# Three more places for the FFN's right operands, and a scratch of 4 KB for dynamic DMAs

## The chip, the cores and the metric

The kernel runs on one core of a Trainium2 chip. The engines are TensorE (PE, its weight loads listed apart as PEld), VectorE (DVE), ScalarE (ACT), GpSimd (POOL) and SyncE (SP, which issues nearly all DMAs). Each engine works through its own queue in order and waits on semaphores. The metric is the time of one execution on the device in microseconds (us); smaller is better.

## The reference

Two layers on a sequence of 1024 tokens with 1024 channels, all in float32. Layer 0 mixes with an mLSTM, layer 1 with a conformer convolution of 31 taps; each is followed by a gated FFN of 2816 channels with a convolution of 3 taps.

```python
c_act = silu(c)
for layer in range(2):
    mod = c_act @ ada_w[layer] + ada_b[layer]
    sh1, sc1, g1, sh2, sc2, g2 = split(mod, 6)
    h = modulate(rmsnorm(x, norm_mix_g[layer]), sh1, sc1)
    y = mlstm_block(h, ...) if layer == 0 else conformer_conv_block(h, ...)
    x = x + g1 * y
    h = modulate(rmsnorm(x, norm_ffn_g[layer]), sh2, sc2)
    x = x + g2 * conv_ffn(h, ...)
return rmsnorm(x, final_g)

def conformer_conv_block(h, ...):
    a, gte = split(h @ w_pw1 + b_pw1, 2)
    u = causal_dwconv(a * sigmoid(gte), dw_w, dw_b)
    return silu(layernorm(u, ln_g, ln_b)) @ w_pw2 + b_pw2

def conv_ffn(h, ...):
    gate, val = split(causal_dwconv(h @ w_up, conv_w, conv_b), 2)
    return (silu(gate) * val) @ w_down
```

## The kernel before

Channels lie on the 128 partitions, in blocks of 128 (`KB` = 8 blocks of the model, `FB` = 22 of the FFN); the 1024 tokens lie along the free axis, in two halves of 512 (`HS`). Every operand of a matmul is split into a high and a low part (`split`, L190: a cast on ACT at L191, a subtraction on DVE at L192), and a product is three matmuls (`PASS`). A split half of 128 x 512 is a tile `h` of 4 KB per partition; a split weight of 128 x 1024 is a tile `wu`. Plain weights (L220) run in the mLSTM, the conformer and a rest of the FFN's down-projection. In the FFN a two-by-two block of products is formed with seven products in place of eight (`Seven`, L507 and L926): its seven right operands are named b11, b21, t1, t3, b22, t2, t4 (`FORMS`), and `ORDER` is the order in which the seven products run, (0, 3, 2, 1, 6, 4, 5), which uses b11, t3, t1, b21, t4, t2, b22.

The stages follow one another: mLSTM (to about 760 us of the profile), FFN of layer 0 (to about 1545), conformer (to about 1934), FFN of layer 1, final norm. The code issues instructions in a program order; a scheduler then orders each engine's queue by priorities and by what it takes to be ready, and the built program holds that order. `tc.high_priority(n)` moves a piece ahead in it. The convolution's taps on DVE (L1725) have `LPC` = -100, so other work of DVE that is ready goes before them.

Memory: pools are put on the left or the right end of the core's SBUF and are closed again. A new tile may be written when the work on what lay at its addresses is over, and a pool that lies on the addresses of an older one makes its first writers wait for the older one's last readers. The scratch for dynamic DMAs is at the bottom of SBUF, 16 KB per partition by default, and all left pools lie above it. POOL issues the DMAs that use it, loads of the band matrices `wband` (L1658).

Three places matter here.

The FFN's right operands. `hx` (L700) has `3 * HALF` = 12 places for tiles `h`; `hpool` has 16. In the up-projection, the 28 tiles of the seven operands fill both. The down-projection's operands are the FFN's own channels, taken in chunks of eight blocks, four pairs. When a product of the last up-projection (L881) or of the last column of a chunk (L944) is issued, `release` (L676) returns the four places of its right operand, and as soon as seven places are free, `forms` (L681) loads one pair (its halves from `p_d`, its sums from `t_d`) and splits its seven operands. `ra` and `rb`, the tiles for the sums, exist once each. Later, `last` (L904) and `place` take further places from the same list.

The adaLN products. `ada_product` (L152) loads 512 KB of `ada_w` and reduces them on DVE (L155 and L156, 128 x 1024) to a column of `mod`; `adas` adds the bias (L162). The last 16 products of layer 1, whose results the FFN of layer 1 needs, run in the conformer from a pool `ca` on the right (`crep1` and two tiles `ada`), which is opened at L1782 behind the conformer's pool `conf`. In the profile these 16 products stand in the second pointwise convolution (pw2, from about 1830 us).

The residual input. `mlstm_down` (L1570) opens `x` again on the right and loads eight blocks (L1575); the right end of the left pools `m2` and `m2w` lies there before.

In the conformer, `cU` (L1677) is a convolution input that goes through a DRAM buffer (`u_d`, L1681 and L1683) to tiles `u` for the convolution on PE (L1703); the other blocks are convolved by the taps on DVE into `cy0` to `cy3`. L1621 and L1629 are the sums of the layer norm, L1633 its root, L1637 its scaling for pw2. L502 is the residual, L272 and L281 the sums of squares of the next norm.

Of the kernel before, what the change touches and what calls it, by code (L numbers as in the profile page):

```python
# [79 lines left out]
def trunk(ctx, tc, a):  # L80
    nc = tc.nc
# [10 lines left out]
    def phase(name, bufs=1, side=None):  # L92
        return tc.tile_pool(name=name, bufs=bufs, side=side, reuse_waits="tile")
# [3 lines left out]
    def nm(s):  # L97
        uid[0] += 1
        return f"{s}_{uid[0]}"
# [149 lines left out]
    class Norm:  # L249
        PARTS = HALVES  # L250

        def __init__(self, x, layer, which):
            self.x, self.layer, self.which = x, layer, which
            self.acts = [[], []]
            self.r = [None] * len(self.PARTS)
            self.squared = [0] * len(self.PARTS)
# [381 lines left out]
    class Operands:  # L638
# [4 lines left out]
        def __init__(self, p_d, t_d, hx):  # L643
            self.p_d, self.t_d, self.hx = p_d, t_d, hx
            self.kept = None
            self.free, self.places, self.right = [], [{}], [None]

        def sums(self, j, g, spare):

# [22 lines left out]
        def release(self, name):  # L672
            self.free += self.places[-2].pop(name)
            right = self.right[-1]
            while len(self.free) >= len(self.FORMS) and len(right["t4"]) < CHUNK // 2:
                self.forms(CHUNK * (len(self.right) - 2) + 2 * len(right["t4"]))  # L676

# [14 lines left out]
    HALF = KB // 2  # L692
    LATER = 16
    CHUNK = 8
    REST = FB - 2 * CHUNK

    def ffn(layer, normed, following, side, other):
        p_d = [dpool.tile([P, S], F32, name=nm("p_d")) for _ in range(FB)]
        with ExitStack() as es_h:
            hx = es_h.enter_context(phase(nm("hx"), 3 * HALF, side=side))  # L700
            t_d = [dpool.tile([P, 2, S], F32, name=nm("t_d")) for _ in range(CHUNK)]
            ops = Operands(p_d, t_d, hx)
            with ExitStack() as es_u:
                ux = es_u.enter_context(phase(nm("ux"), side=side))
                down = ffn_up(layer, normed, p_d, hx, ux, es_u, other, ops)
            open_x(other)
            for k in range(KB):
                dma(x_[0][:, k, :], normed.spill[:, k, :])
            ffn_down(layer, down, p_d, ops, following, other)

    def ffn_up(layer, normed, p_d, hx, ux, es_u, other, ops):
# [21 lines left out]
        def evacuate(j, s, q):  # L733
# [10 lines left out]
            def ready(name, at):  # L744
# [8 lines left out]
                if len(s.ready) == 4:  # L753
                    v.tensor_tensor(s.gate, s.gate, s.val, ALU.mult)
                    dma(p_d[j], s.gate)
                    if j < 2 * CHUNK:
                        ops.sums(j, s.gate, s.val)
# [138 lines left out]
    def ffn_down(layer, forms, p_d, ops, following, other):  # L896
        x = x_[0]
        gate = lambda m: mod[:, layer, 40 + m : 41 + m]
        with phase(nm("dx"), side=other) as dx:
# [4 lines left out]
            def last(h):  # L904
                j = FB - REST + len(acts[h])
                r = raw_tile()[:, :HS]
                dma(r, p_d[j][:, h * HS : (h + 1) * HS])
                t, _ = ops.take()
                split(r, t[:, 0], t[:, 1])
                acts[h].append(t)  # L910
# [4 lines left out]
            for c in range(2):  # L915
                right = ops.right[-1]
                if c == 0:
                    ops.add()
                s = Seven(forms, right, CHUNK // 2)
                s.banks[:4] = [ps() for _ in range(4)]  # L920
# [12 lines left out]
                for m in range(0, KB, 2):  # L933
# [3 lines left out]
                    for n, q in enumerate(ORDER if m else (0, 1, 2, 3, 6, 4, 5)):  # L937
# [16 lines left out]
                        elif q in (1, 6, 5):  # L954
                            ws.load(1 + (1, 6, 5).index(q))
                            if q == 5:
                                ops.free.sort(key=lambda pool: pool is hpool)
                                for _ in range(REST):
                                    last(0)
# [23 lines left out]
            os = [ps() for _ in range(lead)]  # L983
            for k in range(REST):
                for i in range(lead):
                    proj_k(os[i], ws.tiles[i], acts[0], k, REST)
            for h, (c0, c1) in enumerate(LAST if layer == DEPTH - 1 else HALVES):
                for m in range(KB):
# [5 lines left out]
                    following(h, m)  # L994
                    if not h and m >= 1 and len(acts[1]) < REST:
                        last(1)
# [950 lines left out]
```

## Time and profile before

| | us |
|---|---|
| three runs | 2614.78, 2617.64, 2620.78 |
| median | 2617.64 |
| profiled execution | 2619.32 |
| its span, from first to last instruction | 2617.5 |

In the profile a row of a timeline has start, duration, engine, line, operation, output and inputs, shape, count, and in brackets the idle time before it with what released it. A row of a group has line, engine, operation, tiles, shape and count, then busy us and the mean of one in ns, then the idle time before these instructions and its releasers. A row of a stretch has its bounds and length, then busy us (and instructions) of PE, PEld, DVE, ACT and POOL, the clock that PE was granted (1.00 is full), the DMA engines' busy share and GB/s. A DMA row has its queue, count, KB each, and the median us from issue to landing. The mean granted clock of the execution is 0.985.

### The profile page before, as it was taken

What the parts mean: (1) busy time and instruction counts of PE and PEld (TensorE: products, weight loads), DVE (VectorE), ACT (ScalarE), POOL (GpSimd) and SP (SyncE); (2) the same over time, 40 slices, a digit from 0 to 9 for tenths busy, and PEclk for the clock granted to TensorE, in tenths of its full rate; (3) what the DMA queues carried; (4) which work ended last, traced back from release to release, by engine and by line L of the source; (5) the groups of instructions that cost most, each with busy time, mean ns of one, the idle gap of its engine ahead of it and who ended that gap; (6) DMA issues with size and microseconds to landing.
All of it is one profiled execution on the core that took longest, in us unless ns stands there. A gap on an engine that the chain in (4) does not pass through costs nothing.

```text
span 2617.5 us, 31554 instructions
## 1 busy us (share of the span) xinstructions
PE 2501.1 (96%) x11421; PEld 2044.4 (78%) x11421; DVE 2203.5 (84%) x3064; ACT 1329.6 (51%) x2005; POOL 177.4 (7%) x320
## 2 busy tenths in 40 slices
PE   6999899999999999999999999999798999999998
PEld 4788688788778778888877888877576888887787
DVE  8988986787867899998889679992889998888866
ACT  6544445776634554444544342458564444444434
POOL 0232201332100000000000000000000000000000
PEclk9999899999999999999999999999999999999999
DMA  8676355432676234433354331545823332336422
GB/s 306 191 216 206 120 201 185 132 114 70 217 271 215 93 133 161 153 117 101 116 199 148 121 140 50 171 148 165 264 85 117 121 117 101 109 97 219 151 81 97
DMA packets 149085, 393.85 MB, mean 150 GB/s; under 512 B 14848, under 2 KB 36544, under 8 KB 148928
## 3 DMA queue, kind: packets, MB, share of 16 engines
q1 hardware_dynamic: 144320, 372.95, 43.0%
q0 software_dynamic: 4608, 18.88, 2.2%
q8 instruction: 90, 1.47, 0.2%
q14 instruction: 67, 0.55, 0.1%
HBM read 299.46 MB, written 92.31 MB: 150 GB/s over the span
## 4 chain that ended last, share of the span: by engine, by line
PE 67%; DVE 18%; DMA 6%; ACT 6%; issue 3%; SPq 0%; DVEq 0%; ACTq 0%
PE ps L507 41%; PE ps L220 19%; DVE cy L1725 5%; DVE h L192 3%; PE ps L1448 2%; PE ps L1485 2%; DVE wu L192 2%; DMA ada<-in_ada 1%; ACT cy L1712 1%; DMA raw<-xc_d 1%; ACT h L191 1%; PE ps L1102 1%; DMA raw<-p_d 1%; DVE ada L156 1%; ACT wu L191 1%
## 5 line engine op out<-in xcount | busy, mean ns | idle before, releaser
L507 PE MATMUL ps<-h,wu 128*128 128x512 f32 x4704 | 1098.5, 392 | 20.5 <-DVE wu L192 6.8
L507 PEld LDWEIGHTS ps<-h,wu 128*128 128x128 f32 x4704 | 884.1, 189 | 219.9 <-DVE wu L192 10.2
L220 PE MATMUL ps<-h,wu 128*128 128x512 f32 (+1 forms) x2574 | 608.3, 392 | 13.2 <-ACT h L191 6.2
L220 PEld LDWEIGHTS ps<-h,wu 128*128 128x128 f32 x2574 | 480.3, 190 | 122.6 <-ACT h L191 7.8
L191 ACT CAST wu<-raw 128x1024 fp32r<-128x1024 f32 (+1 forms) x286 | 298.4, 1045 | 299.6 <-PE ps L220 89.5
L192 DVE TENSOR_TENSOR wu<-raw,wu 128x1024 fp32r<-128x1024 f32 (+1 forms) x286 | 346.8, 1213 | 69.6 <-ACT wu L191 68.8
L840 DVE SCALAR_TENSOR_TENSOR c<-u,par,c 128x1024 f32<-128x1024 f32 x176 | 219.9, 1279 | 2.5 <-ACT c L838 2.4
L838 ACT ACTIVATE c<-u,par 128x1024 f32<-128x1024 f32 x88 | 108.5, 1243 | 107.5 <-DVE u L627 98.2
L507 PE MATMUL ps<-h,w 128*128 128x512 f32 x648 | 157.3, 390 | 1.9 <-DVE w L192 1.9
L1725 DVE SCALAR_TENSOR_TENSOR cy<-cu,par,cy 128x512 f32<-128x512 f32 (+1 forms) x180 | 156.0, 926 | 1.1 <-ACT cy L1721 0.3
L507 PEld LDWEIGHTS ps<-h,w 128*128 128x128 f32 x648 | 121.5, 188 | 28.0 <-DVE w L192 2.8
L502 DVE SCALAR_TENSOR_TENSOR x<-ps,mod,x 128x512 f32<-128x512 f32 (+1 forms) x140 | 97.9, 715 | 43.3 <-PE ps L220 35.5
L192 DVE TENSOR_TENSOR h<-raw,h 128x512 fp32r<-128x512 f32 (+1 forms) x160 | 105.1, 688 | 25.1 <-ACT h L191 24.9
L191 ACT CAST h<-raw 128x512 fp32r<-128x512 f32 (+1 forms) x160 | 91.4, 605 | 64.7 <-DMA raw<-p_d 28.1
L1448 PE MATMUL ps<-q,h 128*128 128x512 f32 (+2 forms) x576 | 115.3, 349 | 0.3 <-DVE q L192 0.3
L1448 PEld LDWEIGHTS ps<-q,h 128*128 128x128 f32 x576 | 94.9, 189 | 16.0 <-ACT t L1513 2.0
L156 DVE SCALAR_TENSOR_TENSOR ada<-ada,crep 128x1024 f32<-128x1024 f32 x69 | 83.0, 1215 | 22.4 <-DMA ada<-in_ada 22.1
L750 ACT ACTIVATE c<-c 128x1024 f32<-128x1024 f32 x44 | 46.7, 1061 | 94.6 <-DVE c L840 94.5
L728 POOL MEMSET u<- 128x2 f32 x88 | 8.4, 99 | 1123.4 <-DVE c L840 686.6
L220 PE MATMUL ps<-h,h 128*128 128x512 f32 (+1 forms) x450 | 83.6, 347 | 0.0
L220 PEld LDWEIGHTS ps<-h,h 128*128 128x128 f32 x450 | 72.4, 189 | 10.5
L1703 PEld LDWEIGHTS ps<-u,wband 128*128 128x128 f32 x576 | 66.9, 195 | 4.1 <-issue 3.7
(282 smaller groups left out, 3240.0 us busy)
## 6 DMA issues: line engine op xcount, KB each, us to landing
raw<-in_fup SPq DMA_DIRECT2D x94, 512.0 KB, 3.6
ada<-in_ada SPq DMA_DIRECT2D x85, 512.0 KB, 4.6
p_d<-c SPq DMA_DIRECT2D x44, 512.0 KB, 2.7
raw<-in_pw SPq DMA_DIRECT2D x40, 512.0 KB, 3.8
wband<-in_w POOLq DMA_DIRECT2D x32, 576.0 KB, 5.5
raw<-in_mup SPq DMA_DIRECT2D x32, 512.0 KB, 4.4
raw<-in_fdownS SPq DMA_DIRECT2D x32, 512.0 KB, 4.2
raw<-in_mdown SPq DMA_DIRECT2D x24, 512.0 KB, 4.4
```

The lines of the kernel that those rows point to most:

```text
L156: v.scalar_tensor_tensor(w, w, 1.0, crep, ALU.mult, ALU.mult, accum_out=mod[:, layer, b : b + 1])
L191: sc.copy(out_hi, raw)
L192: (engine or v).tensor_tensor(out_lo, raw, out_hi.bitcast(F32), ALU.subtract)
L220: pe.matmul(o, t[:, i, c : c + P], acts[k][:, j, :], start=k == 0 and n == 0, stop=k == nk - 1 and n == 2,)
L502: v.scalar_tensor_tensor(xs, o, gate, xs, ALU.mult, ALU.add)
L507: pe.matmul(o, w[:, i, k * P : (k + 1) * P], acts[k][:, j, :], start=first and k == 0 and q == 0, stop=last and k == n - 1 and q == 2, ski ...
L838: sc.activation(c, body(b), AF.Identity, scale=taps[FK - 1], bias=pv("fcb", layer, b))
L840: v.scalar_tensor_tensor(c, u[b][:, i : i + S], taps[i], c, ALU.mult, ALU.add)
L1448: pe.matmul(so[:, tlo:], xr[cc][I // nJ][:, i, I % nJ * P : (I % nJ + 1) * P], un["qs"][cc][:, j, tlo:], start=n == 0, stop=n == 3 * CB - 1,)
L1485: pe.matmul(un["num"][cc][:, tlo:], vr[I][:, i, cc * P : (cc + 1) * P], pt[:, j, tlo:], start=I == 0 and n == 0, stop=I == nJ * (hf + 1) - ...
L1703: pe.matmul(o, wd[:, 4 * d : 4 * d + 4, :].rearrange("p d c -> p (d c)"), phases[j][:, g, n0 + d : n0 + d + N4], start=d == 0, stop=d == 8,)
L1725: v.scalar_tensor_tensor(y, u[:, t + c0 : t + c1], pv("dww", t, j), y, ALU.mult, ALU.add)
```

## The change

`Operands` starts with three free places of `hx`, the pool `hx` has three places more, and the program is built with a scratch for dynamic DMAs of 4 KB per partition instead of 16.

```diff
-            self.free, self.places, self.right = [], [{}], [None]
+            self.free, self.places, self.right = [hx] * SPARE, [{}], [None]
...
     CHUNK = 8
+    SPARE = 3
     REST = FB - 2 * CHUNK
...
-            hx = es_h.enter_context(phase(nm("hx"), 3 * HALF, side=side))
+            hx = es_h.enter_context(phase(nm("hx"), 3 * HALF + SPARE, side=side))
...
-    nc = bacc.Bacc("TRN2", target_bir_lowering=False, num_devices=1)
+    nc = bacc.Bacc("TRN2", target_bir_lowering=False, num_devices=1, dynamic_dma_scratch_size=4096)
```

The three places take 12 KB per partition, as much as the scratch gives up. Outside the FFN all left pools lie 12 KB lower than before and the right ones stay: `conf`, which reached from 132320 to 189408, ends at 177120, and `ca` begins at 179936, so the two share no address any more. `x` of `mlstm_down`, from 194528 on, no longer lies on the last tiles of `m2` (they end at 184288 instead of 196576), only on `m2w`. Every engine has the same instructions as before in another order; POOL's order is the same too. From line 696 on the new code's numbers are one higher.

DVE at the start of the conformer, before: `gb` is a small product of `mod`, `cu` an input of the taps (L1695), `cy` the taps' sums (L1725), `wu` and `h` are splits.

```order
L1613 TENSOR_TENSOR gb_12592<-mod,par 128x8
L1695 SCALAR_TENSOR_TENSOR cu_12603<-ps_12421,par,t_1873_12601 128x512
L292 SCALAR_TENSOR_TENSOR h_12551<-t_1869_12549,mod,h_12551 128x512
L292 SCALAR_TENSOR_TENSOR h_12562<-t_1871_12560,mod,h_12562 128x512
L192 TENSOR_TENSOR wu_12617<-raw_12615,wu_12617 128x1024
L1695 SCALAR_TENSOR_TENSOR cu_12603<-ps_12423,par,t_1875_12606 128x512
L192 TENSOR_TENSOR wu_12684<-raw_12682,wu_12684 128x1024
```

The same place now, to the first tap:

```order
L156 SCALAR_TENSOR_TENSOR ada_14470,mod<-ada_14470,crep_14433 128x1024
L1614 TENSOR_TENSOR gb_12592<-mod,par 128x8
L156 SCALAR_TENSOR_TENSOR ada_14473,mod<-ada_14473,crep_14433 128x1024
L292 SCALAR_TENSOR_TENSOR h_12551<-t_1869_12549,mod,h_12551 128x512
L292 SCALAR_TENSOR_TENSOR h_12562<-t_1871_12560,mod,h_12562 128x512
L1696 SCALAR_TENSOR_TENSOR cu_12603<-ps_12421,par,t_1873_12601 128x512
L162 TENSOR_TENSOR mod<-mod,par 128x2
L156 SCALAR_TENSOR_TENSOR ada_14478,mod<-ada_14478,crep_14433 128x1024
L156 SCALAR_TENSOR_TENSOR ada_14481,mod<-ada_14481,crep_14433 128x1024
L192 TENSOR_TENSOR wu_12617<-raw_12615,wu_12617 128x1024
L1696 SCALAR_TENSOR_TENSOR cu_12603<-ps_12423,par,t_1875_12606 128x512
L192 TENSOR_TENSOR wu_12684<-raw_12682,wu_12684 128x1024
```

Four of the 16 adaLN products stand there; six more follow among the first six taps, and the last six stand at the end of the taps. Their loads stand on SP directly behind the writes of `x_d`.

DVE in pw2, before: `t` is the layer norm's scaled output, `h` its split form, `x` the residual.

```order
L1637 SCALAR_TENSOR_TENSOR t_2113_14632<-cy_12584,par,csc_12594 128x512
L156 SCALAR_TENSOR_TENSOR ada_14491,mod<-ada_14491,crep_14433 128x1024
L502 SCALAR_TENSOR_TENSOR x_14428<-ps_14606,mod,x_14428 128x512
L156 SCALAR_TENSOR_TENSOR ada_14494,mod<-ada_14494,crep_14433 128x1024
L1637 SCALAR_TENSOR_TENSOR t_2115_14638<-cy_12585,par,csc_12594 128x512
L162 TENSOR_TENSOR mod<-mod,par 128x2
L192 TENSOR_TENSOR h_14635<-t_2113_14632,h_14635 128x512
L192 TENSOR_TENSOR wu_14709<-raw_14707,wu_14709 128x1024
L156 SCALAR_TENSOR_TENSOR ada_14554,mod<-ada_14554,crep_14433 128x1024
L192 TENSOR_TENSOR h_14641<-t_2115_14638,h_14641 128x512
```

The same place now:

```order
L1638 SCALAR_TENSOR_TENSOR t_2113_14632<-cy_12584,par,csc_12594 128x512
L192 TENSOR_TENSOR wu_14653<-raw_14651,wu_14653 128x1024
L1638 SCALAR_TENSOR_TENSOR t_2115_14638<-cy_12585,par,csc_12594 128x512
L1638 SCALAR_TENSOR_TENSOR t_2122_14682<-cy_12586,par,csc_12594 128x512
L1638 SCALAR_TENSOR_TENSOR t_2124_14688<-cy_12587,par,csc_12594 128x512
L192 TENSOR_TENSOR h_14635<-t_2113_14632,h_14635 128x512
L502 SCALAR_TENSOR_TENSOR x_14428<-ps_14606,mod,x_14428 128x512
L192 TENSOR_TENSOR h_14641<-t_2115_14638,h_14641 128x512
```

No adaLN product is left there.

DVE near the end of layer 0's up-projection (about 1280 us in the profile before), now: `w` and `wu` are split weights, the three `h` are the first operands of the down-projection's first pair, split from loads `t`, `raw` and `ra`. Before, the first of them stood nine rows behind `wu_10498`.

```order
L192 TENSOR_TENSOR w_1540_10495<-t_1539_10490,w_1540_10495 128x512
L192 TENSOR_TENSOR h_10568<-t_1548_10560,h_10568 128x512
L192 TENSOR_TENSOR h_10571<-raw_10561,h_10571 128x512
L192 TENSOR_TENSOR h_10574<-ra_10562,h_10574 128x512
L192 TENSOR_TENSOR wu_10473<-raw_10471,wu_10473 128x1024
L569 TENSOR_TENSOR raw_10471<-t_1539_10490,raw_10471 128x512
L570 TENSOR_TENSOR raw_10471<-raw_10471 128x512
L192 TENSOR_TENSOR wu_10498<-raw_10476,wu_10498 128x1024
```

Of the four pairs of a chunk the first three now follow the products with b11, t1 and t4 where they followed those with t3, b21 and t2; the fourth still follows the last release, that of b22. The same holds between the two chunks of the down-projection, and in layer 1.

At the end of the mLSTM, SP's first load of `x` (L1575) stands before the loads of `hn` and `xc` for the operands of block 5, the other seven behind those of block 7; before, all eight stood behind those of block 9. Three of DVE's residuals L502 stand between the splits of those operands.

## The prediction

> **What bounds the kernel now.** I read the page first, then its chain of waits, then a table of stretches, then the timelines of TensorE and VectorE where a stretch is not full.
>
> ```profile
> span 2617.5 us, 31554 instructions
> PE 2501.1 (96%) x11421; PEld 2044.4 (78%) x11421; DVE 2203.5 (84%) x3064; ACT 1329.6 (51%) x2005; POOL 177.4 (7%) x320
> PE 67%; DVE 18%; DMA 6%; ACT 6%; issue 3%; SPq 0%; DVEq 0%; ACTq 0%
> ```
>
> TensorE (PE) is busy 96%, so a change of order can win only its idle time, 116.4 us in all, and the time at a lower clock; it can lose by making PE wait. Of the other third of the chain more than half is VectorE (DVE). The places that this change touches are these:
>
> ```profile
> 1299.00:1335.00 36.00, 30.83 (x119) 22.98 (x118) 33.38 (x47) 19.82 (x30) 0.00 (x0) 0.91 0.74 245
> 1380.00:1412.00 32.00, 30.05 (x125) 22.41 (x125) 30.23 (x46) 20.75 (x35) 0.00 (x0) 1.00 0.67 222
> 1650.00:1660.00 10.00, 7.17 (x47) 6.70 (x46) 10.00 (x12) 4.01 (x7) 0.71 (x2) 0.83 0.33 103
> 1760.00:1830.00 70.00, 66.23 (x385) 56.41 (x384) 22.41 (x26) 52.53 (x93) 4.32 (x9) 0.98 0.45 141
> 1830.00:1900.00 70.00, 53.22 (x193) 37.52 (x191) 57.22 (x90) 37.55 (x50) 0.13 (x2) 0.90 0.80 265
> 2360.00:2402.00 42.00, 35.97 (x139) 27.05 (x138) 37.79 (x53) 22.15 (x33) 0.00 (x0) 0.91 0.76 259
> ```
>
> The columns are PE, PEld, DVE, ACT, POOL busy, then PE's clock, DMA share, GB/s. The first and the last row are the step from up- to down-projection of the two FFNs: PE idles 5.2 and 6.0 us while DVE is 93% and 90% busy. From 1830 to 1900 (pw2 of the conformer) PE idles 16.8 us. At 1650 DVE is full and PE waits; from 1760 on DVE is two thirds idle.
>
> **The change part by part.** Instructions stay the same in number and kind; their order moves. All sums are against the profiled execution (2619.32 us, 1.7 above the median of 2617.64), and I take the difference off the median.
>
> *1. Sixteen products L156 leave the pw2 stage.* The pool `ca` no longer lies on `conf`, so its loads and products needn't wait until the conformer's pools close. Ten now stand at the start of the convolution, six behind most taps.
>
> ```profile
> L156 DVE SCALAR_TENSOR_TENSOR ada<-ada,crep 128x1024 f32<-128x1024 f32 x16 | 19.5, 1218 | 6.4 <-DMA ada<-in_ada 6.3
> L502 DVE SCALAR_TENSOR_TENSOR x<-ps,mod,x 128x512 f32<-128x512 f32 x10 | 7.2, 743 | 0.0
> L192 DVE TENSOR_TENSOR h<-t,h 128x512 fp32r<-128x512 f32 x8 | 5.5, 685 | 0.0
> 1831.78 6.02 PE L220 MATMUL ps<-h,wu 128*128 128x512 f32 x24
> 1837.63 5.31 PE L1629 MATMUL ps<-t,ones 128*128 128x512 f32 x12
> 1845.02 23.24 PE L220 MATMUL ps<-h,wu 128*128 128x512 f32 x100
> 1883.27 4.33 PE L220 MATMUL ps<-h,wu 128*128 128x512 f32 x16 [1.55 <-DVE h L192]
> 1898.67 2.08 PE L281 MATMUL ps<-acc,ones 128*128 128x512 f32 x2 [11.07 <-DVE acc L272]
> 1899.75 34.64 PE L220 MATMUL ps<-h,wu 128*128 128x512 f32 x144
> ```
>
> The group rows are of the window 1830 to 1900. There DVE spends 19.5 us on the products and 6.4 us waiting for their loads, 25.9 in all, and PE's L281 waits for DVE. Without them I ran the new DVE order by hand with the durations of these rows (h split 0.69, residual 0.74; a weight split is 1.22 in the row of 1564 below): the second half's last h split ends at 1868.9, the last sum that L281 needs at 1875.7. PE's own work from 1831.78 is 168 L220 at 0.227 (38.1) and 16 L1629 at 0.45 (7.3), so it gets to L281 at 1877.2 at the earliest, against 1898.67. That is 21.4 us at best. Not less than 16.8, if only the idle time of the stretch goes; I take **20**, as DVE is ready 1.5 us ahead of PE in the hand run, and waits for ACT within the stage will cost about as much.
>
> *2. The ten products are now ahead of the taps.* DVE has little room there:
>
> ```profile
> 1564.34 1.22 DVE L192 TENSOR_TENSOR wu<-raw,wu 128x1024 fp32r<-128x1024 f32 x1 [3.57 <-ACT wu L191]
> 1558.69 0.75 DVE L1695 SCALAR_TENSOR_TENSOR cu<-ps,par,t 128x512 f32<-128x512 f32 x1 [0.57 <-ACT t L1687]
> 1612.05 13.25 DVE L1725 SCALAR_TENSOR_TENSOR cy<-cu,par,cy 128x1024 f32<-128x1024 f32 x11
> ada<-in_ada SPq DMA_DIRECT2D x16, 512.0 KB, 4.8
> 1645.20 1.17 DVE L1677 SCALAR_TENSOR_TENSOR cU<-ps,par,t 128x512 f32<-128x512 f32 x1
> 1653.76 9.78 PE L1703 MATMUL ps<-u,wband 128*128 128x128 f32 x72 [2.83 <-DMA u<-u_d]
> ```
>
> Ahead of the first L1677, on which the first band convolution on PE (L1703) hangs through two DMAs, stand ten products more (12.2), four small biases L162 (an estimated 0.6) and four taps (4.8: eleven in a row take 13.25): 17.6 us. The idle time ahead of the taps (3.57 and 0.57) takes up some; with two `ada` tiles, each third product waits 4.8 us for its load, so by hand only 2.9 is taken up, and L1677 ends at about 1661 instead of 1646.4. PE waited there already, so nothing covers it: the wait of 2.83 grows to about 17. Queued behind it on PE is the rest of the convolution and pw1. The later L1677 have no taps more ahead of them than before, so they are only 8 to 10 us late, and PE, being 14 to 15 late, no longer waits for them. It gets back about 1 of the idle time at 1752, nothing from the 3.77 at 1807, whose work hangs on PE itself:
>
> ```profile
> 1752.09 5.40 PE L1629 MATMUL ps<-t,ones 128*128 128x512 f32 x8 [2.17 <-ACT t L1628]
> 1807.32 10.11 PE L220 MATMUL ps<-h,wu 128*128 128x512 f32 x36 [3.77 <-ACT h L191]
> ```
>
> The six later products cost 7.3 us where DVE has 47.6 of 70 free (1760 to 1830): nothing, unless the last taps become late, which have that whole stretch. Loss **13**, bounds 9 (all idle time filled, the two waits absorbed) and 17 (none filled). Steps 1 and 2 together: **7 faster**, bounds 0 and 12.
>
> A new wait of 14 us also lets the clock fall. The row of 1650 to 1660 shows 0.83 after a wait of 2.83, and the 144 L220 behind the 11.07 took 34.64 where 144 at 0.227 are 32.7. By these rows a long wait costs 1.9 behind it; the old one goes and a new one comes: nothing.
> The Trainium skill ("TensorE: Matmul & The Clock Gate", What's actually happening) says that PE falls to half rate after an idle window of about 3.4 us and needs as long a busy one to return. By it the cost behind a wait is an estimated 1.7, for one of 11 us as for one of 17; the trace's 1.9 agrees, and the slow clock after 2.83 shows that the window's phase counts too.
>
> *3. The FFN's right operands come one release earlier.* With three places free from the start, the first release already frees seven, so `forms` of a pair runs one product earlier, for the first three of the four pairs.
>
> ```profile
> 1282.71 1.23 DVE L192 TENSOR_TENSOR wu<-raw,wu 128x1024 fp32r<-128x1024 f32 x1 [1.60 <-ACT wu L191]
> 1318.13 0.49 PE L926 MATMUL ps<-h,wu 128*128 128x512 f32 x1 [0.37 <-ACT h L191]
> 1320.22 0.73 PE L926 MATMUL ps<-h,wu 128*128 128x512 f32 x2 [1.60 <-DVE h L192]
> 1321.35 0.51 PE L926 MATMUL ps<-h,wu 128*128 128x512 f32 x1 [0.39 <-ACT h L191]
> 1323.83 1.65 PE L926 MATMUL ps<-h,wu 128*128 128x512 f32 x3 [1.98 <-DVE h L192]
> L192 DVE TENSOR_TENSOR h<-rb,h 128x512 fp32r<-128x512 f32 x8 | 5.1, 684 | 1.0 <-ACT h L191 1.0
> L192 DVE TENSOR_TENSOR h<-ra,h 128x512 fp32r<-128x512 f32 x7 | 4.6, 684 | 0.4 <-ACT h L191 0.4
> L926 PE MATMUL ps<-h,wu 128*128 128x512 f32 x36 | 12.1, 447 | 4.3 <-DVE h L192 3.6 <-ACT h L191 0.8
> ```
>
> The group rows are of 1299 to 1335. Three splits (0.6 pitch, 1.8) now fill DVE's gap of 1.60 at 1281, the next pair's loads start sooner, and the gaps of 0.4 and 1.0 that ACT's casts left go. So DVE is about 3 us ahead when L926 begins. In the hand run the four waits of the rows (4.3) vanish, but a wait of about 3 comes for the last pair, which cannot start before the last release and has two weight splits and four taps ahead of it; PE leaves the step 5 us sooner, part of it from fewer matmuls at the low clock. I take half of what is hand-won as lost to landings that I can't see: **3 us per FFN**, and 0.5 each from the same step between the two halves of the down-projection (the stretch from 1380, PE idle 2.0). 7 in all; bounds 0 (the last pair sets the end as now) and 12.
>
> *4. The end of the mLSTM.* `x` no longer lies on the last double weight, so its eight loads stand up to 15 places earlier on SP's queue, seven of them between the loads of `hn` and `xc` for the last operands, and three residuals L502 stand between the splits.
>
> ```profile
> 726.77 0.50 PE L220 MATMUL ps<-h,vr 128*128 128x512 f32 x1 [1.67 <-ACT h L191]
> 753.92 11.41 PE L220 MATMUL ps<-h,wu 128*128 128x512 f32 x49 [1.07 <-DVE wu L192]
> x<-in_x SPq DMA_DIRECT2D x8, 512.0 KB, 9.1
> ```
>
> Against it: three residuals at 0.74, and loads that land later because one of 512 KB goes before them (an eighth of 9.1, 1.1 us) and seven more behind. For it: seven matmuls now stand ahead of the one that waited 1.67, and the split behind the 1.07 no longer waits for a residual. **0**, bounds 3 either way.
>
> *5. The smaller scratch.* It serves the DMAs that POOL issues, the 32 loads of `wband`.
>
> ```profile
> q0 software_dynamic: 4608, 18.88, 2.2%
> wband<-in_w POOLq DMA_DIRECT2D x32, 576.0 KB, 5.5
> L1658 POOL DMA_DIRECT2D wband<-in_w x20 | 10.5, 527 | 195.7 <-PE ps L1703 195.7
> ```
>
> The last row is of 1557 to 1760: POOL waits for PE to free a buffer, not the other way. Cost nothing; were this cover gone, 5.5 us for a load, bound 10 for two in a row.
>
> **Sum.** Conformer 7, FFNs 7, mLSTM 0: 14 us. 2619.3 becomes 2605.3, and from the median 2617.6 comes 2603.6, **2604**.
>
> **The rivals.** *No change (2613 to 2621):* the stall at L1703 is 17 and pw2 gives 17, and in the FFNs the last pair's operands set the end as now, since neither its release nor its DVE work moves. For it speaks that each hand-won microsecond of step 3 hangs on loads into `ra` and `rb`, of which there is one tile each; against it, that DVE has the 1.60, 1.0 and 0.4 to fill and that L926 waits four times for operands which now stand ahead.
> *Slower (about 2623):* ScalarE is the next bound of pw2. Every h form needs a Silu, a cast and then DVE's split, and each sum for L281 a square, all on ACT, which is busy 37.55 of the 70 us. If L281 moves up by only 8 (its 11.07 less some 3 for a residual, a square and a sum in a row), the conformer is 13 - 8 = 5 slower, and with no gain in the FFNs the kernel is at 2623. It decides where pw2 gives less than 13 and the FFNs' gain does not make up the rest. Against it: the 16 products and their waits take 25.9 us off the very engine that L281 waits for, and ACT has 32 us free.
> *The scratch throttles (2620 to 2640):* if a quarter of it holds too few descriptors for the `wband` loads in flight, each L1703 group waits for its own load, up to 5.5 us for each group that isn't covered: four uncovered make 22, and the sum turns to 8 slower. POOL's waits for PE in the row speak against it.
> The Trainium skill ("DMA: Bandwidth & Descriptors", Terms) has these descriptors of 16 bytes written to rings in SBUF, so a smaller ring holds fewer. By it and the 144 packets of a load (4608 / 32), spread over 16 engines, a load is an estimated 144 bytes per engine and direction, and some fourteen loads fit in 4 KB if both directions share it. No run here shows a full ring.
> *The change doesn't do what it says:* excluded for the order, which the rows of the change show; that a place is free and its use is no earlier is the first rival.
>
> **How the numbers follow.** Forecast 0.64, no change 0.20, slower through ACT 0.10, throttled 0.04, and 0.02 for more than 26 us gained. The forecast alone covers 2592 to 2612: 26 is the conformer's 12, the FFNs' 12 and 2 of the mLSTM's 3. The range reaches on to 2618, which takes in three quarters of the first rival and leaves about 2 in 10 outside. A measurement of this kernel tells 0.2% (5.2 us) from no change; the bounds are 2612.4 and 2622.9. Faster is the forecast, the 0.02 and a fifth of the first rival, some of the forecast's own tail taken off: 0.70. Slower is half of the ACT rival, the throttle and a tail of the first: 0.12. Same: 0.18.
>
> **What would show it.** Step 1: no `ada` product between the second half's L1637, L281 some 3 us or less behind the L220 ahead of it. Step 2: ten products between 1557 and 1590, L1677 about 14 us later after the end of the FFN, the wait of the first L1703 at about 17 instead of 2.83, and the other L1703 waiting for nothing. Step 3: the first L192 h of an FFN's last step 13 us sooner, waits of L926 before the last pair gone, the windows of 36 and 42 us shorter by 3 each. Step 4: L220 with `vr` without its wait of 1.67, and L201's weight split not later than before. Wrong would be the prediction if L1703 waits less than 9 or more than 17, if L281 still waits over 6, or if a wait for `wband` shows on PE.

## The result and the profile after

| | us |
|---|---|
| before, median of 4 runs | 2617.51 (2614.78 to 2620.78) |
| the change, median of 4 runs | 2598.85 (2596.91 to 2602.11) |
| ratio, 95% interval | 0.9933 (0.9917 to 0.9949) |
| the change, profiled execution | 2596.91 |
| the change again, on another chip, 5 runs | 2598.65, ratio 0.9936 (0.9924 to 0.9948) |

The change gains 18.7 us (13 to 22 by the interval); 14 were forecast. The ratio is an estimate from all runs of both kernels, not the quotient of the two medians. The two profiled executions lie 22.4 us apart, more than the medians, so what is read from this one pair of traces comes out somewhat too large. The page of the changed kernel answers to the first rows of before:

```profile
span 2595.1 us, 31542 instructions
PE 2489.0 (96%) x11421; PEld 2041.0 (79%) x11421; DVE 2200.3 (85%) x3064; ACT 1328.9 (51%) x2005; POOL 171.3 (7%) x320
```

The 12 instructions fewer are waits and the like in the queues; each engine's own count is the same. TensorE's share still reads 96%. Its idle time fell from 116.4 to 106.1 us, and its busy time fell by 12.1 although it runs the same 11,421 matmuls: more than half of the 22.4 stands in the column that is called busy. Counted over the same matmuls, some 6 us of that are in pw2 and 7 in the four steps of the FFNs; the end of the mLSTM takes 2.7 back. How a wait can hide in busy time is told with the FFN below.

The conformer now, TensorE's timeline from 1630 to 1930 (only rows with a wait ahead of them, and the end of pw2):

```profile
1639.80 10.27 PE L220 MATMUL ps<-h,wu 128*128 128x512 f32 x44 [1.60 <-DVE wu L192]
1662.91 11.17 PE L1704 MATMUL ps<-u,wband 128*128 128x128 f32 x72 [12.85 <-DMA u<-u_d]
1762.39 3.70 PE L1630 MATMUL ps<-t,ones 128*128 128x512 f32 x8 [2.21 <-ACT t L1629]
1815.93 10.13 PE L220 MATMUL ps<-h,wu 128*128 128x512 f32 x36 [3.77 <-ACT h L191]
...
1886.98 1.02 PE L281 MATMUL ps<-acc,ones 128*128 128x512 f32 x2
1887.44 33.25 PE L220 MATMUL ps<-h,wu 128*128 128x512 f32 x144
```

Both sides of the trade are in it. The first band convolution waits 12.85 where it waited 2.83. L281 waits for nothing where it waited 11.07, and the 144 matmuls behind it take 33.25 instead of 34.64. In the table of stretches (columns as before) the 193 matmuls that filled 70 us from 1830 on now stand, but for one, in 49 us, and TensorE idles 0.6 of them. Its busy time fell there from 53.2 to 48.4, and its clock rose from 0.90 to 1.00:

```profile
1838.00:1887.00 49.00, 48.37 (x192) 35.49 (x191) 36.05 (x47) 35.81 (x49) 0.00 (x0) 1.00 0.53 190
```

VectorE's rows say how the products and the first cU came to stand. The columns of the first are those of a group in the stretch 1540 to 1665, the second is of the timeline:

```profile
L156 DVE SCALAR_TENSOR_TENSOR ada<-ada,crep 128x1024 f32<-128x1024 f32 x10 | 12.2, 1220 | 1.3 <-DMA ada<-in_ada 1.3
```
```profile
1654.34 1.08 DVE L1678 SCALAR_TENSOR_TENSOR cU<-ps,par,t 128x512 f32<-128x512 f32 x1
```

The ten products cost 12.2 and only 1.3 of waiting for loads; cU ends at 1655.4, where by hand it was to end at 1661. Half of that difference is only a shift: this stage starts 2.8 us sooner than before, and counted from its start cU is 2.8 us sooner than by hand.

One place had been forecast to neither gain nor lose. At the end of the mLSTM, TensorE now waits for a weight:

```profile
742.59 0.73 PE L220 MATMUL ps<-h,wu 128*128 128x512 f32 x2 [3.83 <-ACT wu L191]
743.85 26.39 PE L220 MATMUL ps<-h,wu 128*128 128x512 f32 x108 [0.53 <-DVE wu L192]
```

VectorE's and ScalarE's timelines there show the chain behind it:

```profile
738.80 0.75 DVE L502 SCALAR_TENSOR_TENSOR x<-ps,mod,x 128x512 f32<-128x512 f32 x1 [4.28 <-PE ps L220]
739.47 0.74 DVE L1566 SCALAR_TENSOR_TENSOR raw<-raw,par 128x512 f32<-128x512 f32 x1
740.25 0.69 DVE L1567 TENSOR_TENSOR raw<-raw,t 128x512 f32<-128x512 f32 x1
...
742.57 1.23 DVE L192 TENSOR_TENSOR wu<-raw,wu 128x1024 fp32r<-128x1024 f32 x1 [0.25 <-ACT wu L191]
```
```profile
740.97 0.62 ACT L191 CAST go<-raw 128x512 fp32r<-128x512 f32 x1 [2.43 <-DVE raw L1567]
741.49 1.04 ACT L191 CAST wu<-raw 128x1024 fp32r<-128x1024 f32 x1
```

A residual (L502) waits 4.28 us for TensorE to finish a group of matmuls. Behind it in VectorE's queue stand L1566 and L1567 for the next operand `go`; on ScalarE the cast of `go` stands ahead of the cast of the weight; and for that weight TensorE then waits. Three queues, each in order, turn a residual that nobody needs soon into a wait of the bound engine.

### The profile page after: what moved, and what is told of

Same layout as the page of the kernel before. It is cut to its first block, busy times and chain, and to the rows that moved or that the text cites. A ratio compares the mean times of both kernels' runs of the same rounds, so it can differ in the third digit from the quotient of the medians.

```text
span 2595.1 us, 31542 instructions
## 1 busy us (share of the span) xinstructions
PE 2489.0 (96%) x11421; PEld 2041.0 (79%) x11421; DVE 2200.3 (85%) x3064; ACT 1328.9 (51%) x2005; POOL 171.3 (7%) x320
## 4 chain that ended last, share of the span: by engine, by line
PE 49%; DVE 14%; ACT 5%; DMA 3%; issue 2%; SPq 0%; DVEq 0%; ACTq 0%
PE ps L507 33%; PE ps L220 14%; DVE cy L1726 3%; DVE wu L192 2%; DVE h L192 2%; DVE c L841 2%; ACT cy L1713 1%; PE ps L1704 1%; ACT wu L191 1%; ACT h L191 1%; DVE x L788 1%; ACT u L1674 1%; DMA raw<-p_d 0%; DMA raw<-in_mdown 0%; DMA x<-in_x 0%
## 5 line engine op out<-in xcount | busy, mean ns | idle before, releaser
L841 DVE SCALAR_TENSOR_TENSOR c<-u,par,c 128x1024 f32<-128x1024 f32 x176 | 219.7, 1280 | 3.3 <-ACT c L839 3.1
L502 DVE SCALAR_TENSOR_TENSOR x<-ps,mod,x 128x512 f32<-128x512 f32 (+1 forms) x140 | 98.5, 716 | 54.6 <-PE ps L220 35.7
L1704 PE MATMUL ps<-u,wband 128*128 128x128 f32 x576 | 68.6, 282 | 12.9 <-DMA u<-u_d 12.9
```

Source lines behind the costliest of these rows:

```text
L502: v.scalar_tensor_tensor(xs, o, gate, xs, ALU.mult, ALU.add)
L841: v.scalar_tensor_tensor(c, u[b][:, i : i + S], taps[i], c, ALU.mult, ALU.add)
L1704: pe.matmul(o, wd[:, 4 * d : 4 * d + 4, :].rearrange("p d c -> p (d c)"), phases[j][:, g, n0 + d : n0 + d + N4], start=d == 0, stop=d == 8,)
```

## The experiments

All times are medians, with the run of before on the same chip. A chip's runs of before spread over 4 to 12 us (21 runs on one chip: 2608.29 to 2620.24), so differences below 3 us are read from the traces, not from the times.

| kernel | us | before | ratio, 95% interval |
|---|---|---|---|
| scratch alone | 2613.35 | 2615.02 | 0.9995 (0.9987 to 1.0004) |
| no places | 2603.66 | 2615.02 | 0.9958 (0.9943 to 0.9972) |
| two places | 2605.02 | 2614.04 | 0.9967 (0.9954 to 0.9979) |
| `ca` on `conf` again | 2607.40 | 2615.02 | 0.9972 (0.9962 to 0.9983) |
| `x` on `m2` again | 2595.36 | 2615.02 | 0.9926 (0.9912 to 0.9939) |
| the change again | 2598.65 | 2614.04 | 0.9936 (0.9924 to 0.9948) |
| products late | 2590.73 | 2614.04 | 0.9906 (0.9892 to 0.9919) |
| products late, `x` on `m2` | 2589.91 | 2614.04 | 0.9909 (0.9894 to 0.9924) |
| four products early | 2590.77 | 2615.56 | 0.9906 (0.9891 to 0.9921) |
| last four later | 2591.99 | 2615.56 | 0.9907 (0.9892 to 0.9922) |
| spread out | 2589.93 | 2615.56 | 0.9896 (0.9880 to 0.9913) |
| spread out, `x` on `m2` | 2586.97 | 2616.61 | 0.9900 (0.9881 to 0.9919) |

Where each one's trace gained and lost is in the next table. Every kernel runs its 11,421 matmuls in almost the same order, so the start of the matmul of the same number can be compared with that in the profile of before; a cell says by how many us the stage was shortened (-) or lengthened (+). The times in the first column are those of before.

| stage | scratch alone | change | change again | no places | two places | `ca` on `conf` | `x` on `m2` | late | spread out | spread out, `x` on `m2` |
|---|---|---|---|---|---|---|---|---|---|---|
| to 700 (same order in all) | -3.4 | -2.1 | -4.3 | -1.1 | -3.1 | -1.5 | -3.6 | -3.3 | -1.7 | -2.6 |
| mLSTM's end, 700 to 770 | 0.9 | 5.0 | 7.1 | 3.3 | 4.5 | 4.6 | 2.1 | 4.6 | 6.0 | 1.6 |
| FFN 0 up to down, 1270 to 1375 | -0.2 | -2.6 | -2.3 | -0.2 | 0.8 | -1.3 | -1.5 | -2.5 | -1.5 | -2.2 |
| FFN 0 between halves, 1375 to 1430 | 0.0 | -2.3 | -2.5 | 1.1 | -0.2 | -2.5 | -1.9 | -2.4 | -1.6 | -2.4 |
| convolution, 1540 to 1825 | -0.5 | 11.4 | 11.9 | 9.9 | 12.1 | -1.4 | 13.1 | 6.9 | 5.4 | 4.1 |
| pw2, 1825 to 1920 | -0.1 | -22.3 | -22.4 | -22.4 | -22.4 | 0.0 | -22.3 | -22.4 | -22.5 | -22.3 |
| FFN 1 up to down, 2345 to 2440 | -3.9 | -5.6 | -3.9 | -4.5 | -1.9 | -4.3 | -4.2 | -5.1 | -5.4 | -4.9 |
| FFN 1 between halves, 2440 to 2500 | -0.9 | -3.3 | -3.7 | 0.3 | -1.7 | -3.7 | -3.1 | -3.7 | -3.2 | -3.2 |

The first row and the column of the scratch alone, whose order is that of before on every engine, show the scatter: the execution that was profiled before was itself 1 to 4 us slow up to 700, and 3.9 us slow in the second FFN.

**The scratch alone.** With `SPARE = 0` in the change as well, 12 KB of unused memory take the place of the scratch:

```diff
-    epst = main.tile([P, 16], F32, name="epst")[:, 0:1]
+    pad = main.tile([P, 3072], F32, name="pad"); epst = main.tile([P, 16], F32, name="epst")[:, 0:1]
```

> Scratch of 4 KB, no spare places, and 12 KB of unused memory in `main`, so that every pool lies where it lay before and every engine has the order of before. Only the ring of POOL's DMAs is smaller. Theory (the ring itself does nothing here): the time of before, 2617 within 3 us, ratio 1.000 within 0.001. Rival (the ring itself moves the time): more than 3 us off on either side; if it throttled the loads of wband, waits for wband on PE and 5 to 22 us more; if a smaller ring were the source of the gain, about 2600.

The ratio is 0.9995, with 1 inside the interval. A ring of 4 KB neither costs nor gains here; the whole change is addresses and places.

**No places.** `SPARE = 0`, with the scratch of 4 KB.

> The change without its three places: pools lie 12 KB lower, `hx` has 12 places, the FFN's operands come when they came before. By my reading of the two traces the lower pools are worth -22.3 in pw2, +11.4 in the convolution and +5.0 at the end of the mLSTM, so -6: 2612 (2608 to 2615), and L926 waits as before. Rival A (the places are all of the gain, the conformer nets nothing): 2617 to 2622. Rival B (the conformer is all of it, the FFNs nothing): 2599.

It gained 11.4, twice the 6 expected, and between the two rivals. The table says that the conformer nets -12.5 here instead of -10.9, and the end of the mLSTM loses 3.3; the rest, up to 700 and in the second FFN, is scatter that the column of the scratch alone has too. It was no clean removal of one part. Without the places ten of the products ran at the end of the first FFN, between 1495.5 and 1554.1 (the likely reason, not tested: the smaller `hx` leaves the addresses of `ca` free sooner). Its trace has the stall at another place:

```profile
1552.91 2.08 PE L281 MATMUL ps<-acc,ones 128*128 128x512 f32 x2 [5.85 <-DVE acc L272]
...
1666.93 9.90 PE L1704 MATMUL ps<-u,wband 128*128 128x128 f32 x72 [4.41 <-DMA u<-u_d]
```

Ahead of TensorE's sum L281 VectorE was late by 5.85, and the band convolution waits only 4.41. Wherever VectorE is full, the products push something back.

**`ca` on `conf` again.** 12 KB of unused memory below `conf`:

```diff
-        cp = cp_es.enter_context(phase("conf", 2))
+        cp_es.enter_context(phase("pad")).tile([P, 3072], F32, name="pad"); cp = cp_es.enter_context(phase("conf", 2))
```

> The change with 12 KB of unused memory below `conf` for as long as `conf` is open, so that `ca` lies on it again, as before, and the 16 products go back into pw2; all else as in the change. Theory (the conformer's two effects net 11): 11 slower than the change, 2610 (2606 to 2613); wait of the first L1704 about 3 instead of 12.85, L281 behind DVE again by about 11. Rival A (they cancel, and the gain is the FFNs'): 2599. Rival B (they are all of the gain): 2617.

The ratio is 0.0037 above the change's, 9.8 us; 11 were expected. Both waits are back as before:

```profile
1653.46 8.28 PE L1704 MATMUL ps<-u,wband 128*128 128x128 f32 x72 [3.35 <-DMA u<-u_d]
...
1896.13 2.08 PE L281 MATMUL ps<-acc,ones 128*128 128x512 f32 x2 [10.75 <-DVE acc L272]
```

So the conformer's part is one address: whether `ca` lies on `conf`.

**Two places.** The pool keeps 15, the list starts with two:

```diff
-            self.free, self.places, self.right = [hx] * SPARE, [{}], [None]
+            self.free, self.places, self.right = [hx] * (SPARE - 1), [{}], [None]
```

> The change with only two of its three places free at the start (the pool keeps its size). The first pair of each step then waits for the second release, as before the change; the second and third pair still come one release earlier. Theory (the first pair's early start is what sets the rest, since the sums of each pair pass through one tile each): most of the 7 us of the FFNs is lost, 4 to 7 slower than the change. Rival (the later pairs count): within 2 of the change.

6.4 slower than the change on the same chip, as the theory had it: with one place fewer the first release gives six places and not seven, the first pair waits for the next. The four FFN rows of the table sum to -3.0, with no places to -3.3, with the scratch alone to -5.0, with the change to -13.8 and -12.4: the third place carries the FFNs' gain. In the view of line L926 (L927 from here on) the columns are min, median and max of one in ns, then the first and the last start. The step between the halves of the second FFN, before, with the change, and with two places:

```profile
L926 PE MATMUL ps<-h,wu x36: 387/389/710, 2456.7 to 2471.4; 128*128 128x512 f32 x36
```
```profile
L927 PE MATMUL ps<-h,wu x36: 387/389/397, 2437.6 to 2448.7; 128*128 128x512 f32 x36
```
```profile
L927 PE MATMUL ps<-h,wu x36: 387/396/501, 2447.2 to 2459.7; 128*128 128x512 f32 x36
```

The starts of the 36 matmuls spread over 14.7, 11.1 and 12.5 us. The longest takes 710 ns before and 397 now; the granted clock in these stretches is 0.92 before and 1.00 with the change and with two places, so a part of what this step won is clock.

**`x` on `m2` again.** 12 KB of unused memory below the mLSTM's pools, closed behind its down-projection:

```diff
-    mkeep = es0.enter_context(phase("mkeep"))
+    es_pad = ExitStack(); es_pad.enter_context(phase("pad")).tile([P, 3072], F32, name="pad"); mkeep = es0.enter_context(phase("mkeep"))
...
-    mlstm_down(stream, spilled, follow(lambda: FfnNorm(0)))
+    mlstm_down(stream, spilled, follow(lambda: FfnNorm(0))); es_pad.close()
```

> The change with 12 KB of unused memory below the mLSTM's pools up to the end of its down-projection, so that the loads of `x` wait for the last double weight again, as before; all else as in the change. Theory (the residuals that now stand between the splits hold up a weight's split: PE's waits of 3.83 for wu go): 5 faster than the change, 2594 (2591 to 2597), the waits of 3.83 and 0.53 for wu at 742 to 744 gone and that of 1.67 for vr back. Rival (the 5 us are scatter between executions, or a loss that the stage would have either way): 2599, within 2 of the change.

The waits are as the theory had them. In place of 3.83 and 0.53 the timeline has:

```profile
723.80 0.50 PE L220 MATMUL ps<-h,vr 128*128 128x512 f32 x1 [2.13 <-ACT h L191]
...
752.39 32.05 PE L220 MATMUL ps<-h,wu 128*128 128x512 f32 x140 [1.07 <-DVE wu L192]
```

The wait of 3.8 at 741 stands in every trace that has the order of the change at the end of the mLSTM, and in none that has the order of before, so it is no chance. The stage lengthens by 3.3 to 7.1 in the new order, by 0 to 2.1 in the old; by the means of the table's columns, before counted as 0, the order costs 3.9 us, not 5. In the times this is not shown: the three kernels with this memory have ratios of 0.9926, 0.9909 and 0.9900, their counterparts 0.9933 and 0.9936, 0.9906, and 0.9896. That the order costs the wait is settled; that it costs the kernel 3.9 us is not.

**The change again.**

> The change itself, on the chip of the next three, as their measure. So far: 18.7 below before (ratio 0.9933). By the four kernels without one part each, it is -11 from the conformer, -7 from the FFNs and 0 to 3 lost at the end of the mLSTM: ratio 0.993 to 0.994 again. Its profile shows which waits of the first one were scatter: the end of the mLSTM should again stand 3 to 5 behind before if the order there costs that (theory), within 1 if it was chance (rival).

Its stages repeat those of the first within about 2 us, the 3.83 and a wait of 12.98 at L1704 among them.

**Products late.** The load of `crep1` waits for the first half's layer norm:

```diff
-        dma(crep, crep_d)
+        sc.copy(crep[:, :2], ys[0][:, :2]); dma(crep, crep_d)
```

> The change with the first two columns of `crep1` written from `cy0` ahead of its load, so that this load and all 16 products wait for the first half's layer norm (about 1740 us) and stand where VectorE has 47 of 70 us free; two columns are copied twice, else the same work. Theory (the ten products ahead of the taps make the first L1704 wait, and pw2 gains because the products are gone from it, wherever they go): the wait of 12.85 falls to about 3 and L281 still doesn't wait: 8 to 11 below the change, 2588 to 2591 at the before of 2617.5. Rival A (VectorE's products and their loads now hold up the taps of cy3 or the weights of the second half there): within 3 of the change. Rival B (the gain of pw2 comes from something else than the products' absence): slower than the change by up to 10.

7.9 below the change on the same chip, just short of the 8 to 11 expected, and below before by 23.3. Rival B is out: pw2 gains its 22.4 wherever the products went. Rival A is half right:

```profile
1649.44 9.90 PE L1704 MATMUL ps<-u,wband 128*128 128x128 f32 x72 [3.54 <-DMA u<-u_d]
...
1801.93 17.37 PE L220 MATMUL ps<-h,wu 128*128 128x512 f32 x64 [8.75 <-DVE wu L192]
```

The stall is gone, and a new one of 8.75 has come behind it, for a weight. VectorE's timeline gives its cause. A late product waits in line for its load, and the weight's split stands behind it:

```profile
1798.85 1.23 DVE L156 SCALAR_TENSOR_TENSOR ada<-ada,crep 128x1024 f32<-128x1024 f32 x1 [4.37 <-DMA ada<-in_ada]
1800.00 0.75 DVE L1670 SCALAR_TENSOR_TENSOR t<-ps,par,t 128x512 f32<-128x512 f32 x1
1800.66 1.22 DVE L192 TENSOR_TENSOR wu<-raw,wu 128x1024 fp32r<-128x1024 f32 x1
```

**Products late and `x` on `m2`.**

> Both edits together: the products late, and 12 KB of unused memory below the mLSTM's pools. If the end of the mLSTM costs 3 to 5 by its order (theory), 3 to 5 below the kernel with late products alone, 2584 to 2587 at the before of 2617.5; if that was chance (rival), the same as it.

The same time within the intervals; it is one of the three pairs above.

**Four products early, last four later, and both.** The tiles of single products are held back in the same manner, by `cy0` or by the last operand of the first half:

```diff
+            if n[0] in (4, 5):
+                sc.copy(w[:, :2], ys[0][:, :2])
+            if n[0] in (12, 13):
+                sc.copy(w[:, :2], s8[0][KB - 1][:, 0, :2])
```

The first condition alone gives four early, on its own with all of `crep1` free; the second, with `crep1` late, gives the last four later; both together, with `crep1` free, are spread out.

> The change with the first four products left where the change puts them and the other twelve held back (the first two columns of their tiles are written from `cy0`, so that they follow the first half's layer norm). Theory (the stall of the first L1704 grows with the DVE work ahead of its cU, and the idle time there takes up the first of it): four products of 1.22 less the 4.1 idle ahead of the taps, so the wait is 4 to 6, against 3.54 with none and 12.85 with ten, and the kernel is 4 to 8 below the change. Rival (the first products cost as much as the later ones, each its 1.22 and a share of its load): wait about 8, 2 to 4 below the change.

The first L1704 (here L1718) waits 4.74: the idle time ahead of the taps does take up most of four products, as the theory had it. The time is that of the late products.

> The kernel with late products, but its last four held back further, until the first half's last operand for pw2 is split, so that they stand in the 11.6 us that VectorE idles there and no longer ahead of the last L1670 and the weight of pw2. Theory (the 8.75 that PE waits for a weight at 1802 there comes from products that wait in line for their loads): that wait falls to 4 or less, the gain of pw2 stays, 3 to 6 below the kernel with late products: 2585 to 2588 at a before of 2617.5. Rival (the weight is late through SP's queue, by loads of any products): the wait stays over 7 and the time as it was.

The wait for the weight fell as expected, from 8.75 to 0.43, and the time didn't move:

```profile
1792.91 6.64 PE L220 MATMUL ps<-h,wu 128*128 128x512 f32 x28 [0.43 <-DVE wu L192]
1807.62 11.02 PE L220 MATMUL ps<-h,wu 128*128 128x512 f32 x36 [8.07 <-ACT h L191]
```

TensorE gets to the next place sooner and waits there 8.07, now for ScalarE: the wait that was taken away came back one place on. (The change waits 3.77 at this place; with late products alone, the 8.75 ahead of it had covered that wait, and the 64 matmuls behind it ran without another.) ScalarE's timeline is full from 1791.75 to 1807, mostly with copies for the last convolution block (L1688) and the evictions of the one before, and only then come the casts of the operands.

> Both: four products early, eight behind the first layer norm, four behind the last operand. If both theories hold, the early four cost 1 to 3 and spare VectorE 5 us later on, where PE then waits for nothing: within 3 of the kernel whose last four are later still. If early products cost their full time: 3 to 6 slower than that.

2589.93, within 1 of the late products; the convolution's stage is the lowest of those without the unused memory (5.4; four early 9.4, last four later 6.9), and the intervals of the four kernels don't part them.

> The kernel with four products early, eight late and four last, with the 12 KB of unused memory below the mLSTM's pools as well: the version that the runs so far point to. By the traces the order at the end of the mLSTM costs 3 to 5 (PE's wait of 3.8 for a weight, in all profiles of the new order and in none of the old). Theory: 3 to 5 below the kernel without the pad (ratio 0.9896): ratio 0.988, 2583 to 2588 at a before of 2617.5, and no wait of 3.8 at 741. Rival (what PE doesn't wait there it waits later on): ratio 0.9895 or more.

The wait of 3.8 is gone and the median is the lowest of all, 29.6 below before. The ratio of 0.9900 is the rival's, but the quotient of the medians is 0.9887 and the interval reaches from 0.9881 on, so these runs don't decide between the two. The kernel beats before and the change, but no better than the others with held-back products do, as far as these runs can tell.

## Why the prediction was right, and where it was not

**The forecast** was 2604 in 2592 to 2618 and faster, and the measured 2598.85 lies inside. Neither rival of the conformer came about: pw2 gave 22 where "no change" needed 17 and ScalarE's rival 8; the scratch did nothing, and POOL's loads still waited for TensorE alone. By the traces the parts are 22.3 - 11.7 + 8.3 - 3.9, 15 in all, against 14 forecast. That these are so near is in part luck: three parts that were each 1 to 2 us better than forecast hide one that was 4 worse. (The 2592 to 2612 that the forecast was said to cover alone has all the good bounds at one end, but not all the bad ones at the other: those sum to 3 us of loss, 2621.)

**Step 1, pw2: 20 forecast, 22.3 measured.** The mechanism held to the row: L281 waits for nothing. From the matmul that starts at 1831.78 in before, L281 now stands 46.6 us behind instead of 66.9, 20.3 sooner and inside the bound of 21.4. The other 2.0 lie behind that: 0.6 in L281 itself, and 1.4 in the 144 matmuls that follow, which take 33.25 instead of 34.64. The prediction had set the second against the new stall, and that set-off is not shown. The first L1704 takes 11.17 behind the 12.85 where it took 9.78, but in the second execution of the change it takes 9.81 behind 12.98:

```profile
1663.65 9.81 PE L1704 MATMUL ps<-u,wband 128*128 128x128 f32 x72 [12.98 <-DMA u<-u_d]
```

And with the order of before it takes 8.28 behind 3.35 (`ca` on `conf`, above) and 11.08 behind 3.06 (the scratch alone).

(The estimate by the Trainium skill, "TensorE: Matmul & The Clock Gate", What's actually happening, was 1.7 for each such wait. The 1.4 of the 144 matmuls is near it; the rows of L1704 don't go with the length of the wait.)

**Step 2, the stall: 13 forecast, 11.4 to 11.9 measured,** the wait 12.85 instead of some 17. The oversized piece is VectorE's work ahead of cU. From the start of the stage (the matmul at 1545.12 in before, 1542.36 now) to the start of cU, VectorE was busy 95.2 of 100.1 us and is busy 110.6 of 112.0. So the work grew by 15.4 where 17.6 were summed, because the records of neighbours overlap (three splits of 0.69 in a row start 0.60 apart), and 3.5 of idle time were taken up where 2.9 were counted; cU is 11.9 late, not 14.7. The loads were priced about right: 1.3 waited for in all, as by hand. The wait grew by 1.9 less than that, 10.0, because TensorE too comes later to L1704, held up on the way by 1.60 for a weight among others. The ten products had been put between 1557 and 1590, and started between 1555.1 and 1583.6.

**Step 3, the FFNs: 7 forecast in all; 6.4 by the times (two places), some 8 by the traces.** The total was right and its parts were not, which is luck. The step from up to down was given 3 in each FFN and gained 1.8 in the first and 0.6 in the second, by the means of the seven columns with three places against those of the scratch alone and of no places; set against the one profile of before, the second seems to gain 5.6. The operands did come sooner: VectorE's first split of them starts at 1283.22 instead of 1294.65. But the wait for the last pair, whose release had not moved and which has four taps ahead of it in VectorE's queue, stayed, as the first rival had it for the FFNs. It is 2.05 in the first FFN, where the longest wait for a split had been 1.98, and in the second, where it had been 1.60:

```profile
2370.72 0.73 PE L927 MATMUL ps<-h,wu 128*128 128x512 f32 x2 [1.75 <-DVE h L192]
```

The step between the halves was given 0.5 and gained 2.8 and 3.1. What failed here was to take TensorE's idle time in a stretch, 2.0 of the 32 us from 1380, as all there was to win. The record of a matmul is longer than its pitch, the distance from one start to the next: in the view of L927 above no matmul's record is shorter than 387 ns, while in an unbroken row one starts every 227. So up to 160 ns of every break between two matmuls show as busy. Counted in matmuls, the stretch of before held 125 of them, 28.4 us at 0.227, so 3.6 were lost. The same stretch now:

```profile
1380.00:1412.00 32.00, 30.91 (x135) 24.67 (x134) 29.84 (x46) 17.04 (x28) 0.00 (x0) 1.00 0.67 227
```

Ten matmuls more in 32 us, 2.3 us, which is what the table has for that step; busy time rose by only 0.9.

**Step 4, the mLSTM's end: nothing forecast, bounds 3 either way; 3.9 lost in the traces.** This is the step that failed in its mechanism. The wait of 1.67 for `vr` shrank as foreseen (0.21 and 1.32 in the two executions), and the sign written down as its mark, a weight's split no later than before, failed. I had priced three residuals at their 0.74 and the loads at their landing. The price that was left out is a residual's own wait for TensorE, 4.28, for everything behind it in the queue.

**Step 5, the scratch: nothing,** as forecast, with the 0.9995 of the kernel that has it alone. The Trainium skill ("DMA: Bandwidth & Descriptors", Terms) has the descriptors of such DMAs written to rings in SBUF, so a smaller ring would hold fewer; no run here, with 32 loads that POOL issues one after the other, shows it full.

## What to carry to other kernels

A pool that moves by 12 KB can move work of whole stages: when two pools stop sharing addresses, the scheduler puts the freed work at the first place where it is ready, not at the first where its engine has time, and holding it back by a dependency on the right tile (here two copied columns) won 7.9 us more. Before pricing an instruction that moves ahead in a queue, look for what it waits for itself: its wait is paid by all behind it. In a stretch where TensorE stutters, count its matmuls against their pitch; its idle time showed 2.0 of 3.6 us lost here.

## What was not expected of the hardware

Two executions of the same order differ by stage, in share, far more than by total: before and the scratch alone differ by 7.8 us in 2617.5, and half of that, 3.9, lies in the 95 us of the second FFN's step. Waits for weights of 1.43 and 0.61 that come and go are part of it:

```profile
2399.77 0.73 PE L507 MATMUL ps<-h,wu 128*128 128x512 f32 x2 [1.43 <-ACT wu L191]
2401.11 4.09 PE L507 MATMUL ps<-h,wu 128*128 128x512 f32 x10 [0.61 <-DVE wu L192]
```

These two rows are of before; the kernel with the scratch alone, in the same order, runs the stretch without them. One profile against one other can misplace 4 us; a control of unchanged order shows where.
